# Expert feed-forward of a two-layer backbone block: whole tiles as two-part operands with three products, and a new split of the experts into rounds

## The chip, the core and the metric

The kernel runs on one core of a Trainium2 chip. The metric is the device time of one execution in microseconds (us), shown as the median of several runs. Engines are named as the profile names them: PE (TensorE, matmuls; PEld its weight loads), DVE (VectorE), ACT (ScalarE), POOL (GpSimd), SP (SyncE, which here issues the large loads). PE's clock has two levels, 1.2 and 2.4 GHz; the profile gives the granted share of the higher one.

## The reference

A block of two layers over 256 latent tokens and 256 context tokens of width 1024, all in 32-bit floats. Each layer mixes tokens and then channels. In the second layer the channel mixer, for the latent tokens alone, is a mixture of eight experts, of which each token uses two:

```python
def swiglu(h, wg, wu, wd):
    return (jax.nn.silu(h @ wg) * (h @ wu)) @ wd

def moe_swiglu(h, router_w, router_b, wg, wu, wd):
    logits = h.astype(jnp.float32) @ router_w.astype(jnp.float32) + router_b.astype(jnp.float32)
    top_val, top_idx = lax.top_k(logits, TOP_K)                     # TOP_K = 2
    ...
    for e in range(N_EXPERTS):                                      # 8
        out = out + gates[..., e:e + 1] * swiglu(h, wg[e], wu[e], wd[e])
```

An expert has three matrices of 1024 x 3584 floats (`wg`, `wu`, and `wd` the other way round), so that the eight experts' weights are 8 x 3 x 1024 x 3584 x 4 bytes = 352.3 MB. They are read once. The change is in this mixture alone.

## The kernel before

All the work up to the router is left as it is. `moe` (in class `K`) computes the router, sorts the experts by how many tokens chose them (expert 0 has most), and hands over to class `Experts`.

**Tiles.** The token slots of the sorted experts are cut into quads of 32 slots. Four quads make a tile of 128 slots; `TILES` (L1323) lists six of them as pairs (expert, first slot). A tile whose four quads belong to one expert is a whole tile; the others are mixed. There are three whole tiles (128 slots of experts 0, 1 and 2) and three mixed ones. `gather` fetches the tokens of three tiles at once by products with a 0/1 matrix `P` and leaves them transposed in `he`, where they serve as PE's stationary operand.

**Rounds, steps, stages and groups.** `ROUNDS` (L1325) puts three tiles into each of two rounds. `ORDER` walks through the four quarters c of the inner width 3584 (896 columns each) and, in each, through round 0 and round 1: eight steps. A `step` has three stages. Gate and up have four groups (i) each; a group loads 256 rows x 896 columns of the quarter for every expert of the round and multiplies them into six PSUM banks `gu`, two per tile. Then the product `a` of both is transposed seven times per tile (`trans`, PSUM tiles `tr`, result `aT`). Down has four groups (u), the last of half size, again into six banks `gu`, which are added to `acc` (128 x 1024 per tile). After the last quarter `back` scales `acc` by the tokens' gates, splits it into two parts `oh` and `ol`, and multiplies these with `PT` back into token order, onto `ymoe` (24 products for three tiles). `end` does the last norm and writes the output.

**Products.** The weights are the moving operand. `products` (L1453) issues, for a whole tile, one 32-bit product per bank of 448 columns (gate, up) or 512 (down), and for a mixed tile four products per bank, one for each quad, on 32 columns of the array each. In the trace a 32-bit product is two matmul instructions.

**What sets the order.** PE's instructions stand as the loops write them (a manual schedule). ACT's and DVE's are placed by a scheduler, and each engine keeps its own order: an instruction that waits holds up those behind it. SP issues the loads in the order of the loops, into a ring of `NW` = 13 buffers `wf` of 8 KB per partition; a load waits until the last reader of its buffer is done, and for the load eight before it. Round 0 loads three experts per group (0, 1, 7), round 1 five (4, 5, 2, 3, 6).

**Elsewhere in the kernel** the two-part form is in use already: `split` (L102) copies a tile into a rounded part `hi` on ACT (L103) and leaves the rest `lo` on DVE (L104), both of the type fp32r, and `mm3` (L106) issues three products, hi x hi, hi x lo and lo x hi (L108 to L110), one matmul instruction each.

Of the kernel before, what the change touches and what calls it, by code (L numbers as in the profile page):

```python
# [1317 lines left out]
class Experts:  # L1318
# [41 lines left out]
    def gather(self, pool, tiles, h2, ps, he):  # L1360

        nc, k, V = self.nc, self.k, self.nc.vector
        n = sum(32 * len(t) for t in tiles)
        P = self.select(pool, tiles)
        for kk in range(8):
            p = ps(kk)
            i = 0
            for t in range(2):
                for part in range(2):
                    k.mm(p[:, 0:n], h2[part][:, t, 128 * kk:128 * kk + 128], P[:, t], i == 0, i == 3)  # L1370
                    i += 1
            if kk % 2:
                V.tensor_copy(he[:, kk], p[:, 0:n])
            else:
                nc.scalar.activation(he[:, kk], p[:, 0:n], AF.Copy)
        out, c = [], 0
        for i, quads in enumerate(tiles):
# [13 lines left out]
            out.append(dict(quads=quads, m=m, he=he[:, :, c:c + m], PT=pt[0:m], g=g[0:m]))  # L1391
# [3 lines left out]
    def start(self, pool, h2, ps):  # L1395
        T = self.k.T
        self.y = T(self.mp, [128, 2, D], "ymoe")
        self.nc.gpsimd.memset(self.y, 0.0)
        self.he = T(self.mp, [128, 2, 8, 384], "he")
        self.tiles = []  # L1400
        for i in range(2):
            self.tiles += self.gather(pool, self.TILES[3 * i:3 * i + 3], h2, ps, self.he[:, i])


    def go(self, ep, pp):
        nc, k = self.nc, self.k
        self.ep, self.pp = ep, pp
        self.ev, self.acc = {}, {}
        rounds = [[self.tiles[i] for i in r] for r in self.ROUNDS]
        with k.tc.manual_schedule(engines={mybir.EngineType.PE}):  # L1410
            for r, c in self.ORDER:
                self.step(rounds[r], c)
        self.end()
        with k.tc.If(nc.values_load(self.en[0:1, 8:9], min_val=0, max_val=8) > 0):
            for quads in self.MORE:
                q, s0 = quads[0]
                cnt = nc.values_load(self.en[0:1, q:q + 1], min_val=0, max_val=S)
                with k.tc.If(cnt > s0):
# [7 lines left out]
                    for c in range(4):  # L1426
                        self.step(tiles, c)
            self.end()

    NW = 13  # L1430
# [14 lines left out]
    def down_weights(self, q, c, u):  # L1445
# [5 lines left out]
        return [w[:, 512 * i:512 * i + 512] for i in range(n)]  # L1451

    def products(self, p, cols, tile, lhs, rhs, first, last):  # L1453

        quads = tile["quads"]
        if len(quads) == 4 and len({q for q, s in quads}) == 1:
            for ps, r in zip(p, rhs[quads[0][0]]):
                self.k.mm(ps[:, 0:cols], lhs, r, first, last)
            return
        for i, ps in enumerate(p):  # L1460
            for j, (q, s0) in enumerate(quads):
                js = slice(32 * j, 32 * j + 32)
                self.k.mm(ps[js, 0:cols], lhs[:, js], rhs[q][i], first, last)

    def step(self, tiles, c):
# [4 lines left out]
        a = [self.T([128, 896], "a", bufs=3) for t in tiles]  # L1470
        for up in range(2):
            ps = banks()
            for i in range(4):
                w = {q: self.up_weights("moe_w_up" if up else "moe_w_gate", q, c, i) for q in experts}
                for t, p in zip(tiles, ps):
                    for kk in range(2):
                        self.products(p, 448, t, t["he"][:, 2 * i + kk], {q: [w[q][kk][:, 448 * s:448 * s + 448] for s in range(2)] for q in w},
                                      i + kk == 0, i + kk == 4)
            for t, p, o in zip(tiles, ps, a):
                m = t["m"]  # L1480
                for s in range(2):
# [12 lines left out]
        for t, p in zip(tiles, ps):
# [85 lines left out]
```

## Time and profile before

| | us |
|---|---|
| median of 3 runs (2483.76 to 2494.44) | 2490.39 |
| the profiled execution, device time | 2495.73 |
| its span, first to last instruction | 2494.0 |
| of it the experts' products, first to last | 1516.6 to 2466.6 |
| of it the last tiles' way back, the norm and the output | 2466.6 to 2494.0 |

The profile is of one execution. Busy times are what an engine's instructions covered. Matmuls overlap in PE, so that what a matmul costs there is the distance from one start to the next, not its duration. A wait in one engine costs something only where that engine holds up the end.

### The profile page before, as it was taken

To read this page: it belongs to the slowest core of one execution; us is meant where nothing else is said; L and a number is where in the kernel's file an instruction comes from. 1 tells how busy PE (TensorE), PEld (TensorE's weight loads), DVE (VectorE), ACT (ScalarE), POOL (GpSimd) and SP (SyncE) were. 2 spreads that over 40 slices of the span, in tenths; PEclk is the share of its full clock that TensorE was granted. 3 is DMA by queue.
4 is the path that set the end of the run, shared out by engine and by line. 5 is a ranking of instruction groups with operands and counts; after the bars stand their busy time and mean duration, and the time that the engine had idled before them with its cause. 6 is when DMAs were issued, how large, how long until landed. Compare 5 with 4: busy or idle time off the path is not lost.

```text
span 2494.0 us, 40273 instructions
## 1 busy us (share of the span) xinstructions
PE 2197.1 (88%) x16243; PEld 1380.5 (55%) x16243; DVE 1024.7 (41%) x2026; ACT 683.9 (27%) x1438; POOL 258.4 (10%) x385
## 2 busy tenths in 40 slices
PE   5898887699799988988776769999999999999996
PEld 2887545577689967767554545433433343334332
DVE  3575758787543436975476651000010101000203
ACT  2643324454433236553432321010100000000001
POOL 4222231220000002020322020000000000000000
PEclk7999968699989989988886769999999999999998
DMA  8764664434433325425653027899979997999795
GB/s 294 205 171 131 201 228 145 123 123 138 137 99 93 94 85 153 145 81 159 214 199 106 31 85 288 316 381 414 407 280 405 415 408 280 406 413 382 270 409 235
DMA packets 320701, 570.49 MB, mean 229 GB/s; under 512 B 25422, under 2 KB 208474, under 8 KB 301562
## 3 DMA queue, kind: packets, MB, share of 16 engines
q1 hardware_dynamic: 303786, 544.46, 60.7%
q10 hardware_dynamic: 12816, 15.42, 1.8%
q0 software_dynamic: 3904, 7.94, 0.9%
q8 instruction: 130, 2.13, 0.4%
q14 instruction: 65, 0.53, 0.1%
HBM read 546.71 MB, written 21.05 MB: 228 GB/s over the span
## 4 chain that ended last, share of the span: by engine, by line
PE 40%; DMA 9%; DVE 5%; ACT 2%; issue 1%; POOL 1%; SPq 0%; ACTq 0%; DVEq 0%; POOLq 0%
PE gu L113 30%; DMA wf<-in_moe_w_down 5%; PE z L113 3%; DMA wf<-in_moe_w_up 2%; DMA lo<-in_ada_w 1%; PE ada L113 1%; PE he L113 1%; PE tr L116 1%; DVE T L1009 0%; DVE itmp L1007 0%; DVE A L999 0%; PE lora L113 0%; PE o L108 0%; PE A L113 0%; PE gu L108 0%
## 5 line engine op out<-in xcount | busy, mean ns | idle before, releaser
L113 PE MATMUL gu<-wf,he 128*32 128x448 f32 (+1 forms) x3840 | 604.2, 542 | 0.2
L113 PEld LDWEIGHTS gu<-wf,he 128*32 128x32 f32 (+1 forms) x3840 | 235.6, 126 | 367.5 <-issue 355.2
L113 PE MATMUL gu<-wf,aT 128*32 128x512 f32 (+1 forms) x1680 | 303.7, 596 | 1.0 <-DMA wf<-in_moe_w_down 1.0
L1484 DVE TENSOR_TENSOR a<-a,gu 128x448 f32<-128x448 f32 x48 | 29.8, 621 | 657.9 <-PE gu L113 655.7
L113 PEld LDWEIGHTS gu<-wf,aT 128*32 128x32 f32 (+1 forms) x1680 | 105.1, 126 | 193.3 <-issue 187.7
L113 PE MATMUL z<-hi,wf 128*128 128x256 f32 x736 | 175.1, 392 | 5.3 <-ACT u L640 5.1
L113 PEld LDWEIGHTS z<-hi,wf 128*128 128x128 f32 x736 | 139.4, 194 | 31.2 <-ACT u L640 5.5
L104 DVE TENSOR_TENSOR wl<-wf,wh 128x512 fp32r<-128x512 f32 (+1 forms) x167 | 128.6, 772 | 61.5 <-ACT wh L103 57.0
L103 ACT ACTIVATE wh<-wf 128x512 fp32r<-128x512 f32 (+1 forms) x167 | 114.5, 688 | 131.9 <-PE gu L109 53.4
L1486 ACT ACTIVATE a<-gu 128x448 f32<-128x448 f32 x48 | 26.0, 543 | 398.5 <-PE gu L113 398.5
L1503 DVE TENSOR_TENSOR acc<-acc,gu 128x512 f32<-128x512 f32 x36 | 24.4, 686 | 225.1 <-PE gu L113 224.9
L1516 ACT ACTIVATE aT<-tr 128x512 f32<-128x512 f32 (+1 forms) x48 | 23.5, 541 | 312.7 <-PE tr L116 312.7
L1557 POOL TENSOR_TENSOR wf<-wf,ol 128x512 f32<-128x512 f32 x2 | 3.3, 1646 | 990.6 <-DVE ol L1556 990.6
L108 PE MATMUL gu<-hi,wh 128*128 128x256 f32 x320 | 96.1, 300 | 7.2 <-ACT wh L103 6.2
L110 PE MATMUL gu<-hi,wl 128*128 128x256 f32 x320 | 96.0, 300 | 5.7 <-DVE wl L104 5.6
L109 PE MATMUL gu<-lo,wh 128*128 128x256 f32 x320 | 93.6, 292 | 0.0
L1009 DVE TENSOR_TENSOR T<-T,itmp 64x31 f32<-64x31 f32 (+15 forms) x248 | 88.2, 356 | 6.1
L104 DVE TENSOR_TENSOR bk<-wf,bk 128x512 fp32r<-128x512 f32 x72 | 49.8, 692 | 96.6 <-ACT bk L103 95.5
L1007 DVE TENSOR_TENSOR itmp<-A,T 64x31 f32<-64x31 f32 (+15 forms) x248 | 84.4, 340 | 5.6
L749 ACT ACTIVATE ltmp<-win,Q 128x128 f32<-128x128 f32 x176 | 64.3, 395 | 63.7 <-DMA win<-zd 20.4
L113 PE MATMUL A<-ar,bk 64*128 64x128 f32 (+1 forms) x512 | 60.7, 308 | 18.3 <-POOL bk L843 16.6
L103 ACT ACTIVATE bk<-wf 128x512 fp32r<-128x512 f32 x72 | 45.3, 629 | 100.1 <-PE gu L109 60.9
(506 smaller groups left out, 3867.2 us busy)
## 6 DMA issues: line engine op xcount, KB each, us to landing
wf<-in_moe_w_gate SPq DMA_DIRECT2D x128, 896.0 KB, 12.3
wf<-in_moe_w_up SPq DMA_DIRECT2D x128, 896.0 KB, 16.4
wf<-in_moe_w_down SPq DMA_DIRECT2D x96, 1024.0 KB, 18.0
wf<-in_w_in SPq DMA_DIRECT2D x75, 512.0 KB, 4.4
lo<-in_ada_w SPq DMA_DIRECT2D x28, 1024.0 KB, 5.6
wf<-in_ffn_w_gate SPq DMA_DIRECT2D x32, 512.0 KB, 3.7
wf<-in_ffn_w_up SPq DMA_DIRECT2D x32, 512.0 KB, 3.8
wf<-in_ffn_w_down SPq DMA_DIRECT2D x32, 512.0 KB, 3.6
```

Source lines behind the costliest of these rows:

```text
L103: self.nc.scalar.activation(hi, src, AF.Copy)
L104: (eng or self.nc.vector).tensor_tensor(lo, src, hi.bitcast(F32), op=OP.subtract)
L108: mm(ps, lhsT=lh, rhs=rh, start=first, stop=False)
L109: mm(ps, lhsT=lh, rhs=rl, start=False, stop=False)
L110: mm(ps, lhsT=ll, rhs=rh, start=False, stop=last)
L113: self.nc.tensor.matmul(ps, lhsT=l, rhs=r, start=start, stop=stop)
L116: self.nc.tensor.transpose(ps, src, self.ident[0:n, 0:n])
L749: self.nc.scalar.activation(tmp[pt], w[pt, 1:129], AF.Copy, scale=self.Q[pt, i:i + 1])
L1007: V.tensor_tensor(tv, A32[:, i + 1:32, i:i + 1].to_broadcast([64, n, m]), T32[:, i:i + 1, 0:m].to_broadcast([64, n, m]), op=OP.mult)
L1009: V.tensor_tensor(T32[:, i + 1:32, 0:m], T32[:, i + 1:32, 0:m], tv, op=OP.subtract)
L1484: V.tensor_tensor(o_, o_, p[s][0:m, 0:448], op=OP.mult)
L1486: nc.scalar.activation(o_, p[s][0:m, 0:448], AF.Silu)
```

## The change

It touches only class `Experts`.

- **Tiles and rounds.** The whole tiles are still the first 128 slots of experts 0, 1 and 2. The mixed ones are now (0, 0, 6, 7), (1, 3, 3, 3) and (4, 4, 5, 5). Round 0 is whole 0, mixed, whole 2 with experts 0, 6, 7, 2; round 1 is mixed, whole 1, mixed with experts 1, 3, 4, 5. Both load four experts per group.
- **Two parts.** `gather` keeps a whole tile's tokens in two parts of type fp32r. A whole tile's weights are split when they are used (`parts`: buffers `wh` and `wl`, three of each), and its `aT` too. `products` then issues three fp32r products in place of one 32-bit product. Mixed tiles are multiplied as before, from the unsplit weights.
- **Buffers.** `NW` goes from 13 to 8.
- **Order.** A bank is evicted right behind its tile's last product, not behind the whole stage. `trans` and the products of `back` are put into a list `todo` and run behind the products of the next tile. `back` takes its parts from `wh` and `wl`.

```diff
-    TILES = [[(0, 0), (0, 32), (0, 64), (0, 96)], [(1, 0), (1, 32), (1, 64), (1, 96)], [(0, 128), (0, 160), (1, 128), (7, 0)],
-    ROUNDS = [(0, 1, 2), (3, 4, 5)]
+    TILES = [[(0, 0), (0, 32), (0, 64), (0, 96)], [(2, 0), (2, 32), (2, 64), (2, 96)], [(0, 128), (0, 160), (6, 0), (7, 0)],
+    ROUNDS = [(0, 2, 1), (4, 3, 5)]
...
-    NW = 13
+    NW = 8
...
+    def parts(self, w, n):
+
+        hi, lo = [self.T([128, 1024], t, F32R, 3)[:, 0:n] for t in ("wh", "wl")]
+        self.k.split(hi, lo, w)
+        return hi, lo
...
     def products(self, p, cols, tile, lhs, rhs, first, last):
-        if len(quads) == 4 and len({q for q, s in quads}) == 1:
-            for ps, r in zip(p, rhs[quads[0][0]]):
-                self.k.mm(ps[:, 0:cols], lhs, r, first, last)
+        if self.whole(quads):
+            for l, r in ((0, 0), (1, 0), (0, 1)):
+                for i, ps in enumerate(p):
+                    mm(ps[:, 0:cols], lhs[l], rhs[r][:, cols * i:cols * i + cols], first and l == r, last and r == 1)
             return
...
     def step(self, tiles, c):
+        turn = lambda t, w, j, n: self.parts(w[t["quads"][0][0]][j], n) if self.whole(t["quads"]) else {q: w[q][j] for q in w}
...
+                for n, (t, p, o) in enumerate(zip(tiles, ps, a)):
+                    late = len(self.todo)
                     for kk in range(2):
+                        self.products(p, 448, t, [x[:, 2 * i + kk] for x in t["he"]], turn(t, w, kk, 896), i + kk == 0, i + kk == 4)
+                    self.flush(late)
+                    if i == 3:
...
+                        if up:
+                            self.todo.append(lambda n=n, t=t, o=o: aT.update({n: self.trans(t, o)}))
...
-            if c == 3:
-                self.back(t, self.acc[key][0:m])
+                    if c == 3:
+                        self.todo += self.back(t, self.acc[key][0:m])
...
     def back(self, t, acc):
+        def products(n, oh, ol):
...
+            oh, ol = [self.T([128, 1024], x, F32R, 3)[:, 0:512] for x in ("wh", "wl")]
...
+            out.append(lambda n=n, oh=oh, ol=ol: products(n, oh, ol))
+        return out
```

How the instructions stand now, at three places.

PE, round 0, gate, first group: the two whole tiles and the first rows of the mixed one. `wf` are weight buffers, `gu` PSUM banks (L113 is the helper `mm`). Before:

```order
L113 MATMUL gu_14023<-wf_14029,he_13800 128x448
L113 MATMUL gu_14024<-wf_14029,he_13800 128x448
L113 MATMUL gu_14023<-wf_14029,he_13800 128x448
L113 MATMUL gu_14024<-wf_14029,he_13800 128x448
L113 MATMUL gu_14025<-wf_14040,he_13800 128x448
L113 MATMUL gu_14026<-wf_14040,he_13800 128x448
L113 MATMUL gu_14025<-wf_14040,he_13800 128x448
L113 MATMUL gu_14026<-wf_14040,he_13800 128x448
L113 MATMUL gu_14027<-wf_14029,he_13800 32x448 x2
L113 MATMUL gu_14027<-wf_14040,he_13800 32x448
```

Now, the same place up to the mixed tile:

```order
L113 MATMUL gu_14108<-wh_14158,he_2610_13801 128x448
L113 MATMUL gu_14109<-wh_14158,he_2610_13801 128x448
L113 MATMUL gu_14108<-wh_14158,he_2611_13802 128x448
L113 MATMUL gu_14109<-wh_14158,he_2611_13802 128x448
L113 MATMUL gu_14108<-wl_14159,he_2610_13801 128x448
L113 MATMUL gu_14109<-wl_14159,he_2610_13801 128x448
L113 MATMUL gu_14108<-wh_14168,he_2610_13801 128x448
L113 MATMUL gu_14109<-wh_14168,he_2610_13801 128x448
L113 MATMUL gu_14108<-wh_14168,he_2611_13802 128x448
L113 MATMUL gu_14109<-wh_14168,he_2611_13802 128x448
L113 MATMUL gu_14108<-wl_14169,he_2610_13801 128x448
L113 MATMUL gu_14109<-wl_14169,he_2610_13801 128x448
```

A whole tile's four 32-bit products of a group have become twelve fp32r products, the last two of each six from the part that DVE makes, and the mixed tile comes next instead of the second whole tile.

ACT, the end of the first gate stage. `a` is the result of the stage, made from the banks of the three tiles in turn. Before:

```order
L1486 ACTIVATE a_14020<-gu_14023 128x448
L1486 ACTIVATE a_14020<-gu_14024 128x448
L1486 ACTIVATE a_14021<-gu_14025 128x448
L1486 ACTIVATE a_14021<-gu_14026 128x448
L1486 ACTIVATE a_14022<-gu_14027 128x448
L1486 ACTIVATE a_14022<-gu_14028 128x448
```

Now (L103 is the first half of `split`; `wh_14390` and `wh_14400` are the second whole tile's weights of the last gate group, `wh_14426` and later those of the up stage):

```order
L1516 ACTIVATE a_14105<-gu_14108 128x448
L1516 ACTIVATE a_14105<-gu_14109 128x448
L1516 ACTIVATE a_14106<-gu_14110 128x448
L103 ACTIVATE wh_14390<-wf_14348 128x896
L103 ACTIVATE wh_14400<-wf_14348 128x896
L1516 ACTIVATE a_14106<-gu_14111 128x448
L103 ACTIVATE wh_14426<-wf_14418 128x896
L103 ACTIVATE wh_14436<-wf_14418 128x896
L1516 ACTIVATE a_14107<-gu_14112 128x448
L1516 ACTIVATE a_14107<-gu_14113 128x448
```

The splits of the weights that the second whole tile needs now stand behind an eviction that waits for the mixed tile's first bank.

PE, round 0, last quarter: where the way back of the first tile (`tr<-...PT`) stands. Before:

```order
L113 MATMUL gu_17502<-wf_17593,aT_17485 32x512 x2
L113 MATMUL gu_17502<-wf_17595,aT_17485 32x512
L113 MATMUL gu_17502<-wf_17597,aT_17485 32x512
L113 MATMUL tr_17617<-oh_17613,PT_13871 128x512
L113 MATMUL tr_17617<-ol_17614,PT_13871 128x512
L113 MATMUL tr_17621<-oh_17613,PT_13871 128x512
L113 MATMUL tr_17621<-ol_17614,PT_13871 128x512
```

Now:

```order
L113 MATMUL gu_19531<-wf_19745,aT_19514 32x512
L113 MATMUL tr_19777<-wh_19761,PT_13913 128x512
L113 MATMUL tr_19777<-wl_19762,PT_13913 128x512
L113 MATMUL tr_19781<-wh_19761,PT_13913 128x512
L113 MATMUL tr_19781<-wl_19762,PT_13913 128x512
L113 MATMUL tr_19785<-wh_19765,PT_13913 128x512
L113 MATMUL tr_19785<-wl_19766,PT_13913 128x512
L113 MATMUL tr_19789<-wh_19765,PT_13913 128x512
L113 MATMUL tr_19789<-wl_19766,PT_13913 128x512
L113 MATMUL gu_19532<-wh_19803,aTh_19562 128x512
```

Before, all 24 products stood behind the step's last product; now the first tile's eight stand between the mixed tile's last product and the second whole tile's last ones, whose weights come from the same ring `wh`.

## Rows read from the trace of the kernel before

**Rows 1.** The page: busy time by engine, and two lines of slices:

```profile
PE 2197.1 (88%) x16243; PEld 1380.5 (55%) x16243; DVE 1024.7 (41%) x2026; ACT 683.9 (27%) x1438; POOL 258.4 (10%) x385
PE   5898887699799988988776769999999999999996
DMA  8764664434433325425653027899979997999795
```

**Rows 2.** Busy us by stretch: PE, PEld, DVE, ACT, POOL; PEclk, DMA share, GB/s:

```profile
1752.60:1868.60 116.00, 115.25 (x581) 47.57 (x581) 7.09 (x11) 6.79 (x13) 0.00 (x0) 1.00 0.86 339
1868.60:1988.10 119.50, 118.36 (x853) 43.20 (x845) 7.92 (x13) 6.20 (x12) 0.00 (x0) 1.00 1.02 410
2339.80:2350.10 10.30, 7.31 (x28) 3.65 (x24) 10.01 (x17) 2.89 (x4) 0.00 (x0) 1.00 0.99 393
2466.60:2494.00 27.40, 7.38 (x28) 3.62 (x24) 17.27 (x27) 7.14 (x15) 3.29 (x2) 0.75 0.12 42
```

**Rows 3.** The same view: round 0's gate and up, its down; then round 1's:

```profile
1752.60:1827.40 74.80, 74.80 (x388) 31.13 (x384) 3.01 (x5) 3.86 (x7) 0.00 (x0) 1.00 1.01 405
1831.40:1868.60 37.20, 37.20 (x174) 13.59 (x176) 3.36 (x5) 0.86 (x2) 0.00 (x0) 1.00 0.58 214
1868.60:1944.90 76.30, 76.23 (x581) 27.36 (x573) 3.83 (x7) 3.26 (x6) 0.00 (x0) 1.00 1.03 406
1949.00:1988.10 39.10, 38.78 (x253) 12.99 (x252) 3.43 (x5) 0.74 (x2) 0.00 (x0) 1.00 1.01 416
```

**Rows 4.** Matmuls in 32 bits: min/median/max ns; whole tiles in order of time (start, us):

```profile
L113 PE MATMUL gu<-wf,he x3840: 538/539/644, 1516.6 to 2424.6; 128*32 128x448 f32 x148, 128*128 128x448 f32 x44
L113 PE MATMUL gu<-wf,aT x1680: 592/592/697, 1596.0 to 2466.1; 128*32 128x512 f32 x146, 128*128 128x512 f32 x41
1564.46 5.42 PE L113 MATMUL gu<-wf,he 128*128 128x448 f32 x14
1596.82 5.74 PE L113 MATMUL gu<-wf,aT 128*128 128x512 f32 x13
```

**Rows 5.** Busy time by stretch, earlier: fp32r products of 512, then 256 columns:

```profile
741.20:763.40 22.20, 22.20 (x97) 17.95 (x97) 9.13 (x15) 7.06 (x14) 0.00 (x0) 1.00 0.31 94
763.60:808.40 44.80, 44.80 (x384) 44.80 (x383) 16.26 (x29) 15.21 (x31) 0.00 (x0) 1.00 0.31 95
```

**Rows 6.** Groups by line and shape: xcount | busy us, mean ns | idle before:

```profile
L103 ACT ACTIVATE wh<-wf 128x512 fp32r<-128x512 f32 x144 | 90.5, 629 | 110.3 <-PE gu L109 53.4 <-PE dn L110 27.9 <-PE o L110 8.4
L103 ACT ACTIVATE wh<-wf 128x1024 fp32r<-128x1024 f32 x23 | 24.1, 1051 | 21.5 <-PE z L109 21.5
L104 DVE TENSOR_TENSOR wl<-wf,wh 128x512 fp32r<-128x512 f32 x144 | 100.4, 699 | 42.6 <-ACT wh L103 38.3 <-POOL u L689 3.2
L104 DVE TENSOR_TENSOR wl<-wf,wh 128x1024 fp32r<-128x1024 f32 x23 | 28.2, 1230 | 18.8 <-ACT wh L103 18.8
```

**Rows 7.** The same view, from 1510 us on: evictions and way back:

```profile
L1486 ACT ACTIVATE a<-gu 128x448 f32<-128x448 f32 x48 | 26.0, 543 | 398.5 <-PE gu L113 398.5
L1503 DVE TENSOR_TENSOR acc<-acc,gu 128x512 f32<-128x512 f32 x36 | 24.4, 686 | 225.1 <-PE gu L113 224.9
L1533 DVE TENSOR_TENSOR ymoe<-ymoe,tr 128x512 f32<-128x512 f32 x24 | 15.3, 678 | 0.6 <-PE tr L113 0.6
L1527 DVE SCALAR_TENSOR_TENSOR ol<-acc,gs,oh 128x512 fp32r<-128x512 f32 x12 | 8.9, 744 | 0.0
L1526 ACT ACTIVATE oh<-acc,gs 128x512 fp32r<-128x512 f32 x12 | 8.7, 722 | 78.8 <-DVE acc L1503 65.9 <-PE tr L113 12.6
```

**Rows 8.** Loads from 1495 us on: KB each, median us to landing:

```profile
wf<-in_moe_w_gate SPq DMA_DIRECT2D x128, 896.0 KB, 12.3
wf<-in_moe_w_down SPq DMA_DIRECT2D x96, 1024.0 KB, 18.0
```

**Rows 9.** The first loads, 1495 to 1530 us, and one wait of SP (longest last):

```profile
DMA to landing us min/median/max: 4.8/12.9/17.5
SPq L1442 <- PE he L113: 14.5, 1, 14.5
```

More of the change, by code (lines that the diff above doesn't have):

```diff
@@ L1390, in gather @@
             V.tensor_copy(g[0:m], p[0:m, 256:257])
-            out.append(dict(quads=quads, m=m, he=he[:, :, c:c + m], PT=pt[0:m], g=g[0:m]))
+            rows = [x[:, :, c:c + m] for x in parts] if self.whole(quads) else [he[:, :, c - nw:c - nw + m]]
+            out.append(dict(quads=quads, m=m, he=rows, PT=pt[0:m], g=g[0:m]))
             c += m
@@ L1398, in start @@
         self.nc.gpsimd.memset(self.y, 0.0)
-        self.he = T(self.mp, [128, 2, 8, 384], "he")
         self.tiles = []
         for i in range(2):
-            self.tiles += self.gather(pool, self.TILES[3 * i:3 * i + 3], h2, ps, self.he[:, i])
+            tiles = self.TILES[3 * i:3 * i + 3]
+            n = sum(map(self.whole, tiles))
+            he = T(self.mp, [128, 8, 384 - 128 * n], f"he{i}")
+            parts = [T(self.mp, [128, 8, 128 * n], f"he{i}{j}", F32R) for j in range(2)]
+            self.tiles += self.gather(pool, tiles, h2, ps, he, parts)
     def go(self, ep, pp):
@@ L1462, in products @@
                 js = slice(32 * j, 32 * j + 32)
[L1463 removed]
+                mm(ps[js, 0:cols], lhs[0][:, js], rhs[q][:, cols * i:cols * i + cols], first, last)
     def step(self, tiles, c):
@@ L1515, in trans @@
                 k.tr(p[:, m * j:m * j + m], a[0:m, j0 + j::7], m)
[L1516 to L1517 removed]
+            src = p[:, 0:m * n].rearrange("p (j m) -> p j m", m=m)
+            if whole:
+                k.split(o[0][:, j0:j0 + n, 0:m], o[1][:, j0:j0 + n, 0:m], src)
+            else:
+                nc.scalar.activation(o[0][:, j0:j0 + n, 0:m], src, AF.Copy)
+        return [x[:, :, 0:m] for x in o]
     def back(self, t, acc):
         nc, V, m = self.nc, self.nc.vector, t["m"]
[L1522 removed]
+        def products(n, oh, ol):
             ns = slice(512 * n, 512 * n + 512)
[L1524 to L1527 removed]
             for h in range(2):
@@ L1533, in back @@
                 V.tensor_tensor(self.y[:, h, ns], self.y[:, h, ns], p, op=OP.add)
+        out = []
+        for n in range(2):
+            ns = slice(512 * n, 512 * n + 512)
+            oh, ol = [self.T([128, 1024], x, F32R, 3)[:, 0:512] for x in ("wh", "wl")]
+            nc.scalar.activation(oh[0:m], acc[:, ns], AF.Copy, scale=t["g"])
+            V.scalar_tensor_tensor(ol[0:m], acc[:, ns], t["g"], oh[0:m].bitcast(F32), op0=OP.mult, op1=OP.subtract)
+            out.append(lambda n=n, oh=oh, ol=ol: products(n, oh, ol))
+        return out
     def end(self):
```

102 lines of the change are left out of this document (57 added, 45 removed).

## The prediction

> **What bounds the kernel now.** I read the page first [rows 1]. From the 25th slice on, which is the experts' part, PE is at 9 tenths throughout; the line of DMA below it swings there between 5 and 9. So in this part PE is the bound and the loads have room, at least in some stretches. The view by stretch [rows 2] shows in which. Round 0's step of the second quarter takes 116.0 us at 339 GB/s, round 1's 119.5 us at 410 GB/s with a DMA share of 1.02; the other three quarters are pairs of the same kind. PE is busy for all but one us of each. Stage by stage [rows 3], round 1 takes 1.5 us longer in gate and up (76.3 against 74.8) and 1.9 us in down (39.1 against 37.2), with as many products: these 3.4 us are the waits for loads, since round 1 loads five experts and round 0 three. So a pair of steps is 232 us of PE work and some 3.4 us of waits. Loads alone, at 410 GB/s, would need 88.1 MB / 410 = 215 us a pair. PE is the bound, and the loads stand 17 us below it.
>
> **What the change does to PE.** Starts of 32-bit products lie (5.42 - 0.54) / 13 = 0.376 us apart at 448 columns and (5.74 - 0.59) / 12 = 0.429 us at 512 [rows 4], from the stretch less the last one's own length (0.539 and 0.592 us, same rows). A product is two of them: 0.752 and 0.858 us. fp32r products lie 22.2 / 96 = 0.231 us apart at 512 columns and 44.8 / 384 = 0.117 us at 256 [rows 5]; between them, at 448, 0.203 us. Three cost 0.608 and 0.694 us. A whole tile has 32 bank products in gate and up and 14 in down per step, so it saves 32 x 0.144 + 14 x 0.164 = 6.9 us, of some 36. A mixed tile is left as it is. Round 0 keeps two whole tiles and round 1 one, so that the PE work of a step falls from 116.0 to 102.2 us in round 0 and from 116.1 to 109.2 in round 1: 83 us over four quarters, if nothing else ended later.
>
> The Trainium skill ("FP8 and Floating Point Precision", TensorE Precision Notes) says that true FP32 takes four passes through the array; three of four would save 9.0 us per whole tile and step, 25 us more in all than the rows give. The rows decide: 0.608 is 0.81 of 0.752, not 0.75. By the page the time would be some 8 us lower, because only round 1 is still paced by PE.
>
> **The loads.** Both rounds now load four experts: 44.0 MB a step, at 410 GB/s [rows 2] 107.4 us. That is more than round 0's PE work and a little less than round 1's. So the new split takes the waits out of round 1 and makes the loads the pace of round 0. The ring has 8 buffers in place of 13, two groups of four. In round 0 a group is whole, mixed, whole; its PE work is 2 x 2.43 + 3.0 + 0.3 = 8.2 us (the 0.3 is what 74.8 us [rows 3] hold beyond 96 products of 0.752, over eight groups) against 3.67 MB / 410 = 9.0 us for the loads. Experts 0, 6 and 7 are held until the mixed tile is done, 5.7 us into the group, and expert 2 until DVE has split it. A single load took 4.8 us from issue to landing at the least [rows 9], and each that queues behind it 2.2 us more. So the three land 10.5, 12.7 and 14.9 us into the group, or 2.2 later behind an earlier load of expert 2, and are wanted two groups on: the first at 16 us (18 less its split), the others at 20.6, behind the whole tile. That leaves 3 us or more, and the loads can keep running; but 3 us is not much, and stalls of both sides will meet.
>
> **Splits.** A pass of 896 columns is copied by ACT and subtracted by DVE. Between the rows for 512 and 1024 columns [rows 6] that is 0.95 and 1.10 us; at 1024 1.05 and 1.23. PE uses a pass of 896 for 6 x 0.203 = 1.22 us, so that DVE alone would just keep up, and in a group of round 0 it has 4 x 1.10 = 4.4 us of work in 9. They are hidden by the mixed tile and by three buffers, wherever the order lets them run ahead. Where it doesn't, PE waits. At the end of round 0's gate the second whole tile's split stands behind an eviction of the mixed tile's first bank; that bank ends 0.75 us before the tile, the eviction takes 0.54 [rows 7], the split 0.95, then DVE's 1.10: 1.1 us late at the end. Likewise 0.6 us at the end of down, and at the start of each round 0 the evictions into `acc` (0.69 each) hold up DVE's first split by 1.0 us. Scattered transposes add changes between PE's modes: taken as 0.6 us in round 0 and 0.5 in round 1. So 2.3 us in round 0 and 1.5 in round 1.
>
> **The steps.** Round 0: PE 104.5, loads 107.4; I take 107.4. Round 1: PE 110.7, plus half of the 3.4 us that the waits cost where loads run at full rate: 112.4. Half, because PE and not DMA is the longer there, but by little. A pair is 219.8 us, four are 879.2.
>
> **Ways back.** Before, 24 products with their waits took 10.3 us after round 0 and as much of the tail after round 1 [rows 2]. Now they lie between other tiles. Round 0: 24 x 0.231 = 5.5 us of PE, and 4 us in which the second whole tile's last weights wait for the ring `wh`: PE must release the first tile's parts, which need two additions, two `ol` and two `ymoe` on DVE [rows 7], then ACT and DVE split. Together 9.5, so nothing is won there. Round 1: 16 x 0.231 = 3.7 us and 3.7 us of the same wait. Sum 16.9 us.
>
> **Start and tail.** The first product waits for `gather`, as before; its columns are the same in number (1536 per slice of the width), so I leave 1516.6 us and add 1.5 for the first split, whose DVE half stands behind the last copies of `gather`. Before, SP's second load waited 14.5 us for `gather` [rows 9]; now the first eight loads wait for buffers that are free by then, so that two groups are there when PE begins. That is no gain by itself, since PE is not waiting there. Tail: of the 27.4 us [rows 2] 11.0 were three ways back; one is left, bound by DVE: 2 x 0.69 + 2 x 0.74 + 4 x 0.68 = 5.6. So 22.0.
>
> **Sum.** 1516.6 + 1.5 + 879.2 + 16.9 + 22.0 = 2436.2 us of span, against 2494.0. The profiled execution took 1.7 us more than its span, so 2437.9, and lay 5.3 us above the median of the runs: **2433**.
>
> **Rivals.**
> *Clean overlap.* If cushions hold everywhere and only the loads pace round 0 and only PE round 1, a pair is 107.4 + 109.2: 13 us less, 2420. If even the loads are hidden, PE's 211.4 a pair is all: 34 less, 2399. For it: round 1 of before lost only 3.4 us in twelve groups with its loads at full rate. Against: that was with 13 buffers.
> *Exposed splits.* If the loads come just in time, each group's first split lies open: 0.95 + 1.10 us less the four high products (0.81), 1.24 us. In the 46 groups of one round that is 57 us: 2490, no change; in a quarter of them, 2447. Against: the 3 us above, and ACT and DVE are at half load.
> *Too few buffers* (the slower side). A buffer's cycle is its use, its landing and its split: 5.7 + L + 2.05 us, and it must fit into two groups, 18 us. The median landing was 12.3 us for gate and 18.0 for down [rows 8], because eight loads queue in SP's ring; if L stays 13 with the ring of 8, a group takes 10.4 us, 1.0 over its mean of 9.3 (107.4 / 11.5), and 92 groups cost 95 us: 2528. It decides from L = 12 us on, where the 57 us are gone. Against: with four buffers in use only four can queue, and L is 4.8 to 9.2.
> *It doesn't do what it says.* If fp32r products of 448 columns between 32-column tiles cost as much as the two 32-bit ones, nothing is saved: pairs of 118.3 + 119.3, 2504.
> *Slow loads.* Busy stretches move 405 to 416 GB/s [rows 3]; if four experts a group ran at the 339 of round 0's whole step, each step would be 130 us: 2594. That 339 holds idle time (214 in down, 0.58 busy), so I give it 0.01. The Trainium skill ("DMA: Bandwidth & Descriptors", Specifications) puts a core's share of HBM at about 358 GB/s, which would make the weights alone 984 us, longer than the stage is now; the trace disagrees, with 410 over 119.5 us.
>
> **How the numbers follow.** Forecast 0.65, with 2412 to 2456 as its own range (from near-clean overlap to 3.4 us of waits in each step). Clean overlap 0.12, exposed splits 0.12, too few buffers 0.07, no saving 0.03, slow loads 0.01. The range takes in most of clean overlap and the first part of exposed splits: 2402 to 2482. Half a per cent is about what a measurement of this kernel can tell: faster means under 2478, slower over 2503. Faster: 0.65 + 0.12 + 0.06 = 0.83; same 0.07, from exposed splits and part of no saving; slower 0.10.
>
> **What would show it.** In the trace after: starts of fp32r products of 448 columns 0.20 us apart; steps near 107 and 112 us in place of 116.0 and 119.5; a DMA share near 1.0 in both rounds; loads from 1500 us on without a gap; a stall of some 4 us before the last products of round 0's second whole tile; the end 22 us behind the last product of `gu`. It is wrong if PE waits over 0.5 us per group on `wh`, `wl` or `wf`, if landing takes over 12 us, or if DMA falls well under 400 GB/s inside a stage.

## The result and the profile after

| | before | after |
|---|---|---|
| median, us | 2488.6 (2483.76 to 2494.44, 4 runs) | 2426.89 (2414.86 to 2437.87, 4 runs) |
| ratio, 95% interval | | 0.975 (0.9707 to 0.9793) |
| profiled execution: span | 2494.0 | 2418.1 |
| first product of the experts at | 1516.6 | 1504.6 |
| products of `gu`, first to last | 950.0 | 888.5 |
| tail behind them | 27.4 | 25.0 |

The changed kernel takes 2427 us; 2433 was forecast. Of the 75.9 us between the two spans, 12.0 lie ahead of the experts' first product, where the two kernels differ in `gather`, the first split and the start of the loads (10507 and 10540 matmul instructions), and the last section shows that this part differs from one execution of the same kernel to the next. So the reading below goes by what is called the stage from here on, from the first product of `gu` to the end of the span: **977.4 us before, 913.5 after**, 63.9 less.

The page after; it answers to [rows 1]:

```profile
PE 2112.2 (87%) x16827; PEld 1483.1 (61%) x16827; DVE 1336.8 (55%) x2342; ACT 939.5 (39%) x1730; POOL 258.8 (11%) x385
PE   4898877799879988988965677999999999999996
DMA  8765574444433316434655024999999999999994
```

Before, the DMA line swung between 7 and 9 in the experts' part (the 5 is the last slice, which holds the tail); now it stands at 9 from the 26th slice to the last but one (the experts begin at the end of the 25th). PE's line reads the same as before, and that is the trap of this case. The steps of the second quarter, those of the last, and the tail, by stretch, with the columns of [rows 2]:

```profile
1723.90:1829.59 105.69, 103.91 (x666) 64.07 (x666) 58.36 (x61) 49.66 (x60) 0.00 (x0) 1.00 1.02 408
1829.59:1940.49 110.90, 110.90 (x896) 53.41 (x895) 33.94 (x38) 27.27 (x35) 0.00 (x0) 1.00 1.02 405
2158.36:2275.41 117.05, 111.81 (x686) 69.04 (x682) 67.86 (x76) 50.99 (x63) 0.00 (x0) 0.97 1.02 407
2275.41:2393.13 117.72, 114.70 (x913) 53.84 (x912) 41.73 (x50) 30.72 (x39) 0.00 (x0) 0.99 0.85 332
2393.13:2418.10 24.97, 6.13 (x16) 3.38 (x16) 13.96 (x21) 5.76 (x13) 3.20 (x2) 0.65 0.12 46
```

A pair of steps is 216.6 us in place of 235.5. By the first two rows round 1 looks as if PE were its bound: busy for all of 110.90 us. The runs show that it isn't.

Products of 448 columns stand as forecast, six in 1.21 us, by the timeline of one whole tile (start, length, instructions):

```profile
1514.58 0.97 PE L113 MATMUL gu<-wh,he 128*128 128x448 f32 x4
1515.38 0.57 PE L113 MATMUL gu<-wl,he 128*128 128x448 f32 x2
1515.79 0.97 PE L113 MATMUL gu<-wh,he 128*128 128x448 f32 x4
```

### The profile page after: what moved, and what is told of

Its sections match the earlier page's. It is cut to its first block, busy times and chain, and to the rows that moved or that the text cites. A ratio compares the mean times of both kernels' runs of the same rounds, so it can differ in the third digit from the quotient of the medians.

```text
span 2418.1 us, 42430 instructions
## 1 busy us (share of the span) xinstructions
PE 2112.2 (87%) x16827; PEld 1483.1 (61%) x16827; DVE 1336.8 (55%) x2342; ACT 939.5 (39%) x1730; POOL 258.8 (11%) x385
## 4 chain that ended last, share of the span: by engine, by line
PE 39%; DMA 8%; DVE 7%; ACT 4%; issue 2%; POOL 1%; SPq 0%; ACTq 0%; DVEq 0%; POOLq 0%
PE gu L113 28%; DMA wf<-in_moe_w_up 5%; PE z L113 3%; DVE wl L104 1%; ACT wh L103 1%; DMA lo<-in_ada_w 1%; PE he L1372 1%; DMA win<-zd 1%; PE tr L116 1%; PE gu L108 1%; ACT ltmp L749 1%; DVE T L1009 1%; PE gu L110 0%; DVE itmp L1007 0%; PE gu L109 0%
## 5 line engine op out<-in xcount | busy, mean ns | idle before, releaser
L104 DVE TENSOR_TENSOR wl<-wf,wh 128x896 fp32r<-128x896 f32 (+2 forms) x443 | 430.9, 994 | 494.1 <-ACT wh L103 481.1
L103 ACT ACTIVATE wh<-wf 128x896 fp32r<-128x896 f32 (+2 forms) x443 | 374.2, 869 | 562.9 <-DMA wf<-in_moe_w_up 158.0
L113 PE MATMUL gu<-wf,he 128*32 128x448 f32 x3072 | 314.5, 542 | 0.1
L113 PEld LDWEIGHTS gu<-wf,he 128*32 128x32 f32 x3072 | 107.6, 110 | 172.9 <-issue 157.0
L113 PE MATMUL gu<-wh,he 128*128 128x448 f32 x768 | 194.6, 375 | 4.6 <-ACT wh L103 4.0
L113 PE MATMUL z<-hi,wf 128*128 128x256 f32 x736 | 176.4, 394 | 5.7 <-ACT u L640 5.5
L113 PEld LDWEIGHTS gu<-wh,he 128*128 128x128 f32 x768 | 139.5, 188 | 60.9 <-issue 27.3
L113 PEld LDWEIGHTS z<-hi,wf 128*128 128x128 f32 x736 | 140.2, 195 | 32.0 <-ACT u L640 6.1
L113 PE MATMUL gu<-wf,aT 128*32 128x512 f32 x1344 | 151.7, 595 | 0.0
L113 PE MATMUL gu<-wl,he 128*128 128x448 f32 x384 | 111.9, 373 | 3.5 <-DVE wl L104 2.9
L113 PEld LDWEIGHTS gu<-wf,aT 128*32 128x32 f32 x1344 | 40.0, 110 | 89.8 <-issue 87.8
L103 ACT ACTIVATE bk<-wf 128x512 fp32r<-128x512 f32 x72 | 45.3, 629 | 100.1 <-PE gu L109 60.9
L113 PEld LDWEIGHTS gu<-wl,he 128*128 128x128 f32 x384 | 70.8, 189 | 16.1 <-DVE wl L104 10.6
L113 PE MATMUL A<-ar,bk 64*128 64x128 f32 (+1 forms) x512 | 56.6, 298 | 20.5 <-POOL bk L843 17.5
## 6 DMA issues: line engine op xcount, KB each, us to landing
wf<-in_moe_w_up SPq DMA_DIRECT2D x128, 896.0 KB, 12.9
wf<-in_moe_w_down SPq DMA_DIRECT2D x96, 1024.0 KB, 12.3
```

The source lines that it names most:

```text
L103: self.nc.scalar.activation(hi, src, AF.Copy)
L104: (eng or self.nc.vector).tensor_tensor(lo, src, hi.bitcast(F32), op=OP.subtract)
L113: self.nc.tensor.matmul(ps, lhsT=l, rhs=r, start=start, stop=stop)
```

## The experiments

The time of the second quarter's steps, of `gu` and of the stage come from one profile each; times with an interval come from interleaved runs, and their ratio is to the kernel before in the same series (2488.6 to 2498.0 us). e3_two leaves out one product of three; e4_half and e11_order_half load about half of the weights.

| | time, us | ratio (95%) | steps of the second quarter, round 0 and 1 | gu | stage |
|---|---|---|---|---|---|
| before | 2488.6 | | 116.0, 119.5 | 950.0 | 977.4 |
| after | 2426.9 | 0.975 (0.9707 to 0.9793) | 105.7, 110.9 | 888.5 | 913.5 |
| e10_after, after once more | 2429.8 | 0.974 (0.9708 to 0.9771) | 105.9, 110.9 | 886.8 | 911.0 |
| e1_products | 2485.1 | 0.9977 (0.9949 to 1.0004) | 101.2, 129.5 | 946.0 | 970.3 |
| e2_split | 2488.5 | 0.9995 (0.9965 to 1.0024) | 116.3, 116.6 | 946.9 | 974.2 |
| e3_two | 2410.9 | one run | 106.0, 110.2 | 871.3 | 895.9 |
| e4_half | 2391.8 | one run | 100.9, 108.5 | 858.9 | 883.3 |
| e5_ring6 | 2475.4 | 0.9909 (0.9877 to 0.9940) | 113.2, 114.9 | 926.5 | 950.5 |
| e6_order | 2454.9 | 0.9855 (0.9791 to 0.9919) | 111.8, 114.7 | 911.5 | 939.9 |
| e7_before_ring8 | 2539.7 | one run | 116.0, 130.9 | 993.3 | 1020.6 |
| e8_back | 2425.5 | 0.973 (0.9683 to 0.9776) | 105.8, 110.6 | 881.8 | 906.2 |
| e9_spread | 2432.2 | 0.973 (0.9698 to 0.9763) | 105.7, 110.9 | 881.2 | 906.1 |
| e11_order_half | 2436.6 | one run | 104.5, 110.4 | 875.5 | 903.8 |

### Each part alone

The products without the new split (in the changed kernel):

```diff
-TILES: [0 x4] [2 x4] [0 0 6 7] | [1 x4] [1 3 3 3] [4 4 5 5]
+TILES: [0 x4] [1 x4] [0 0 1 7] | [2 x4] [4 4 5 5] [3 3 3 6]
 ROUNDS = [(0, 2, 1), (4, 3, 5)]
```

> The changed kernel with the old split of the tiles: round 0 holds experts 0, 1 and 7 with two whole tiles, round 1 the experts 4, 5, 2, 3 and 6 with one; products, ring, order as changed. Bytes: 33.0 MB in a step of round 0, 55.05 MB in one of round 1. Theory (the prediction's: PE saves 20.7 us a pair, but only the new split lets the loads follow): round 0 is PE's, 104 to 105 us; round 1 is the loads', 55.05 MB / 410 = 134 us, less what the ring of eight has loaded ahead (up to 8 x 2.2 us, of which I take 6), 128; a pair 232 against the changed kernel's 218, so about 2484, no change against before. Rival (the products alone do it, the split is decoration): a pair of 104.5 + 111 = 215.5, 2425.

The new split without the products (in the kernel before):

```diff
-TILES: [0 x4] [1 x4] [0 0 1 7] | [4 4 5 5] [2 x4] [3 3 3 6]
+TILES: [0 x4] [2 x4] [0 0 6 7] | [1 x4] [1 3 3 3] [4 4 5 5]
-ROUNDS = [(0, 1, 2), (3, 4, 5)]
+ROUNDS = [(0, 2, 1), (4, 3, 5)]
```

> The kernel before with the new split and order of the tiles alone: both rounds load four experts; 32-bit products, 13 buffers, transposes and ways back as before. Theory: PE stays the bound with 116 us a step in both rounds, and only round 1's 3.4 us of waits for loads go: steps of 116 and 116.3, 13 us in all, about 2475. Rival (the waits come from the 410 GB/s that round 1 has anyway, and stay): steps 116 and 119.5, 2488. Rival (the split is the larger part of the gain): under 2460.

By stretch, round 0 and round 1 of the second quarter, first of e1_products, then of e2_split:

```profile
1770.33:1871.57 101.24, 101.20 (x665) 64.14 (x665) 60.10 (x61) 51.13 (x59) 0.00 (x0) 1.00 0.89 341
1871.57:2001.05 129.48, 119.58 (x897) 53.52 (x896) 33.63 (x38) 26.45 (x35) 0.00 (x0) 1.00 1.02 410
```

```profile
1748.78:1865.07 116.29, 115.53 (x578) 47.35 (x574) 7.17 (x11) 6.79 (x13) 0.00 (x0) 1.00 0.95 377
1865.07:1981.64 116.57, 115.81 (x850) 41.78 (x849) 7.85 (x12) 6.19 (x12) 0.00 (x0) 1.00 0.98 381
```

The first came out as the theory had it, 2485 for 2484. Round 0 wins 14.8 us with its cheaper products, and round 1 loses 9.9: at 410 GB/s and a share of 1.02 it can only wait for its five experts, while the loads stand still for a tenth of round 0. The second removes round 1's waits (119.5 to 116.6) and is then held by PE in both rounds. Its first step took 121.7 us, so that the stage is 3.2 us shorter and the time unchanged within its interval; 2475 was expected. Alone the parts bring 7.1 and 3.2 us of the stage (the second is hardly more than the 2.4 by which the stage of one kernel differs between two executions, e10_after), together 63.9. Each takes away one of two bounds that lie close together. But the parts are not taken apart cleanly: e1_products keeps the changed kernel's order and its ring of 8 buffers, and 8 buffers alone cost the kernel before 43 us with this old split (e7_before_ring8, below). What the products would bring with the old split and 13 buffers, no run shows.

### What paces the rounds now

Less work for PE, then fewer bytes (both in the changed kernel):

```diff
-            for l, r in ((0, 0), (1, 0), (0, 1)):
+            for l, r in ((0, 0), (1, 0)):
```

> The changed kernel with two products in place of three for whole tiles: the product of the activations' high part with the weights' low part is left out (the splits are still made). PE has 9.7 us less work per whole tile and step: 19.4 us in round 0, 9.7 in round 1. Theory (loads pace round 0, PE round 1): round 0 stays at 106 to 108 us, round 1 falls from 111 to the loads' 107; the products of gu span 888.5 - 16 = 872 us. Rival B (loads pace both rounds already): both stay, 885 to 889. Rival C (PE, with its waits for splits, paces both): round 0 falls to 87, round 1 to 101, 773.

```diff
-        src = ...[256 * i:256 * i + 256, ...]; dma_start(v, src...); return [v[:, 0], v[:, 1]]
+        src = ...[256 * i:256 * i + 128, ...]; dma_start(v[:, 0], src); return [v[:, 0], v[:, 0]]
```

> The changed kernel with about half the bytes: each load of gate and up brings only its first 128 rows, each of down its first 1024 columns, and they are used twice, so that PE, ACT and DVE do all that they did. 23.1 MB a step in place of 44.0, some 57 us of transfer. Theory: round 0 falls from 106.5 to PE's 102.2 + 2.3 of stalls = 104.5, round 1 from 111.3 to 110.7, or to 109.5 if waits for loads are in it; the products of gu span 875 to 880 us. Rival B (loads pace both rounds): round 1 falls by as much as round 0, both by 3 us or more, under 865. Rival C (splits and order pace both): both stay, 885 to 889.

The second quarter's steps of e3_two, then of e4_half:

```profile
1724.11:1830.14 106.03, 95.20 (x577) 46.40 (x574) 57.06 (x60) 48.15 (x60) 0.00 (x0) 1.00 1.02 409
1830.14:1940.39 110.25, 106.60 (x850) 42.63 (x850) 34.80 (x39) 28.68 (x37) 0.00 (x0) 1.00 1.02 408
```

```profile
1717.65:1818.59 100.94, 100.94 (x669) 64.21 (x665) 59.23 (x60) 51.12 (x60) 0.00 (x0) 1.00 0.68 231
1818.59:1927.09 108.50, 108.50 (x896) 50.27 (x895) 35.31 (x39) 28.79 (x36) 0.00 (x0) 1.00 0.63 212
```

With 29 us less PE work in a pair, the pair takes 216.3 us in place of 216.6. So the loads pace **both** rounds: rival B by the steps of e3_two, although its `gu` of 871.3 is the 872 of the theory, by another way. The steps of 105.7 and 110.9 run at nearly the same rate and differ in where the border falls (105.69 x 408 = 43.1 MB against 110.90 x 405 = 44.9, together the pair's 88.0). Of the 17.2 us that `gu` did lose, 14.0 are in the first step (101.2 for 107.3) and the last (109.8 for 117.7); in these two the loads of after stand at a share of 0.94 and 0.85. e4_half gives PE's own pace: 100.9 and 108.5, 209.4 a pair, 7 us below the loads' (with the order of ACT and DVE that the scheduler made for it, of which more below). Its `gu` of 858.9 is rival B's (under 865), but round 1 falls by 2.4 us, not by the 3 or more that B wanted.

That ACT and DVE with their splits are not the pace either shows in what ACT waited for in after, from 1500 us on (us in total, times, longest):

```profile
ACT wh L103 <- DMA wf<-in_moe_w_up: 158.0, 40, 8.1
ACT wh L103 <- DMA wf<-in_moe_w_gate: 118.5, 31, 8.3
ACT wh L103 <- DMA wf<-in_moe_w_down: 79.7, 23, 8.0
```

Why did PE look busy in round 1? The last mixed tile of one group and the first of the next (64 instructions in a row), by the timeline, in after, in e4_half and in e3_two:

```profile
1853.91 6.57 PE L113 MATMUL gu<-wf,he 128*32 128x448 f32 x64
```

```profile
1833.19 6.22 PE L113 MATMUL gu<-wf,he 128*32 128x448 f32 x64
```

```profile
1855.89 7.27 PE L113 MATMUL gu<-wf,he 128*32 128x448 f32 x64
```

The same work takes 6.22 us in all seven such places of e4_half's step, 6.5 to 6.9 us in after's and 7.3 to 8.2 in e3_two's. Mixed tiles need no split and PE's order is the same in after and e4_half, so the difference is the wait for a late load, and in after all of it counts as busy: it lies between the products and leaves no idle time. The seven places together are 2.6 us longer in after than in e4_half, the step 2.4.

The idle time that the profile does name is another matter. The waits of PE in the second quarter of after (waits by engine and line: us in total, times, longest):

```profile
PE gu L113 <- ACT wh L103: 1.4, 2, 0.7
PE gu L113 <- DVE wl L104: 0.6, 1, 0.6
```

In e4_half that list is empty for the same quarter. That doesn't make them waits for late loads, since the scheduler places ACT's and DVE's instructions anew for each kernel, and in e4_half it has put the splits earlier. The two waits on ACT, at the start of round 0's step and at the end of its gate, in after:

```profile
1722.41 0.60 ACT L1536 ACTIVATE acc<-gu 128x512 f32<-128x512 f32 x1 [0.17 <-PE gu L113]
1722.91 1.78 ACT L103 ACTIVATE wh<-wf 128x896 fp32r<-128x896 f32 x2
1723.90 1.09 PE L113 MATMUL gu<-wh,he 128*128 128x448 f32 x4 [0.70 <-ACT wh L103]
1753.96 0.54 ACT L1516 ACTIVATE a<-gu 128x448 f32<-128x448 f32 x1 [1.65 <-PE gu L113]
1754.40 1.78 ACT L103 ACTIVATE wh<-wf 128x896 fp32r<-128x896 f32 x2
1755.40 1.07 PE L113 MATMUL gu<-wh,he 128*128 128x448 f32 x4 [0.75 <-ACT wh L103]
```

The second place in e4_half (the later of the second whole tile's two last splits of the gate, and the mixed tile's first eviction):

```profile
1744.58 0.95 ACT L103 ACTIVATE wh<-wf 128x896 fp32r<-128x896 f32 x1 [0.26 <-PE gu L113]
1747.41 0.54 ACT L1516 ACTIVATE a<-gu 128x448 f32<-128x448 f32 x1 [1.01 <-PE gu L113]
```

In after both splits start the moment that the eviction ahead of them is done, and the load for the first (issued at 1711.5 us, landed 6.3 us later) had been there for 5 us. These are waits for ACT's order. The third, of 0.59 us on DVE at the start of down, is not taken apart here. They do not set the pair's length, which e3_two keeps.

### The ring

```diff
-    NW = 8
+    NW = 6
```

> The changed kernel with 6 buffers in the ring of the loads in place of 8. Theory (the prediction's rival of too few buffers, with its own rule): use 5.7 us + landing + splits 2.05 us must fit into 6/4 of a group; with landings of 4.8 to 9.2 us a group takes 8.4 to 11.3 us, 9.8 in the middle, 0.75 over the 9.05 us that a group now takes; over 92 groups +70 us, about 2497. Rival (the ring is deep enough, the 407 GB/s alone set the pace): steps as in the changed kernel, 2427 to 2435.

And the kernel before:

```diff
-    NW = 13
+    NW = 8
```

> The kernel before with 8 buffers in its ring in place of 13. Theory: round 1's loads need 134 us for 116 us of PE work, and what closes the gap is what 13 buffers hold in advance, 29 us; with 8 it is 17.6, 11 us less, so that round 1's steps go from 119.5 to 130 and round 0's stay at 116: +42 us, about 2532. Rival (the ring does not matter where PE is the bound): steps of 116 and 119.5, 2490.

The second quarter, of e5_ring6 and of e7_before_ring8:

```profile
1743.53:1856.71 113.18, 109.21 (x665) 65.66 (x666) 58.08 (x61) 48.35 (x59) 0.00 (x0) 1.00 0.99 391
1856.71:1971.61 114.90, 112.76 (x896) 55.17 (x895) 34.44 (x39) 27.38 (x37) 0.00 (x0) 1.00 0.98 383
```

```profile
1764.21:1880.21 116.00, 115.25 (x578) 47.57 (x577) 7.06 (x11) 6.79 (x13) 0.00 (x0) 1.00 0.78 298
1880.21:2011.12 130.91, 123.39 (x854) 45.47 (x846) 7.96 (x13) 6.19 (x12) 0.00 (x0) 1.00 1.02 410
```

Two buffers fewer cost 37 us of stage (950.5 for 913.5), half of what the rival's rule gave: the rate falls from 406 to 387 GB/s. In the kernel before, 8 buffers cost 43 us, 42 expected: five experts a group need more than 8 (what lies between 8 and 13 was not tried). With 8 buffers and the new products the old split takes 970.3 us of stage (e1_products), the even one 913.5. So the change could give up five buffers because its rounds are even.

### The order

Transposes between up and down, ways back behind the whole step, as before; then the same with half the bytes:

```diff
-                    self.flush(late)          # behind each tile's products
+        self.flush()                          # once, behind up
+        for t in tiles: self.todo += self.back(t, ...); self.flush()     # c == 3, behind down
```

> The changed kernel with the old places of transposes and ways back: all transposes of a step between its up and its down, all ways back behind the whole step; split, products and ring as changed. Theory (after the runs with half the loads and with two products: both rounds go at the pace of the loads, and PE has 5.3 us of room in round 0 and 2.4 in round 1): the exposed wait of the last tile's transposes and of the first tile's split costs 2 to 3 us a step, of which room hides half; 8 x 1.2 = 10 us; way back of round 0 as before 10.3; round 1's 6.4 leaves its step, but the tail grows by two ways back, 9 us; together +12, about 2439. Rival (loads hide it all): +3, 2430. Rival (nothing is hidden): 8 x 3 + 3 = +27, 2454.

> The run with the old places of transposes and ways back, with about half the bytes as in the run with half the loads. Theory (a wait of PE between up and down fills the ring, the loads stop, and what they lose is not caught up, since they set the pace): PE alone takes 100.9 + 3.1 of wait + some 3 us at half clock = 106 to 107 us in round 0 and 110 in round 1, both under the 111.6 and 113.5 with all the bytes, and round 0's under the loads' own 107.4. Rival (the wait is PE's, and PE is the bound): as with all the bytes, 111 to 113.

e6_order at its border of up and down, by the timeline (in brackets the idle time before and its releaser), and two stretches:

```profile
1807.25 3.59 PE L116 MATMUL tr<-k_ident,a 128*128 128x128 f32 x14 [3.07 <-DVE aTl L104]
```

```profile
1807.20:1813.00 5.80, 5.70 (x20) 4.81 (x21) 2.27 (x4) 3.53 (x6) 0.00 (x0) 0.50 1.02 424
1831.00:1841.00 10.00, 10.00 (x64) 5.74 (x66) 3.86 (x4) 3.24 (x4) 0.00 (x0) 1.00 0.52 187
```

e11_order_half, second quarter:

```profile
1747.66:1852.19 104.53, 101.47 (x670) 64.22 (x666) 59.23 (x60) 51.39 (x61) 0.00 (x0) 1.00 0.67 223
1852.19:1962.58 110.39, 109.03 (x896) 50.27 (x895) 35.22 (x39) 28.48 (x35) 0.00 (x0) 1.00 0.63 208
```

The old order costs 26.4 us of stage, all of what the rival "nothing is hidden" gave; my 12 fell. PE alone needs 104.5 and 110.4 in that order, 214.9 a pair and still less than the loads' 216.3, yet with all the bytes the pair takes 226.5. The rows show how: PE waits 3.07 us, runs the next 5.8 us at a granted clock of 0.50 (the lower level), and some 18 us later the loads are down to a share of 0.52 for 10 us. What the loads lose there is not made up, because they are the pace. My 106 to 107 for round 0 counted that half clock in; with half the bytes the clock stayed at 1.00 in that quarter. That the idle loads are the buffers that PE held longer is inferred from the order of events, not tried by itself; e11_order_half, like e4_half, has its own order of ACT and DVE too.

### The ways back

One lent buffer of the ring holds the parts of a way back:

```diff
-            oh, ol = [self.T([128, 1024], x, F32R, 3)[:, 0:512] for x in ("wh", "wl")]
+            oh, ol = b[:, 1024 * n:1024 * n + 512], b[:, 1024 * n + 512:1024 * n + 1024]    # b: one "wf"
```

> The changed kernel with the parts of a way back in a buffer of the ring of the loads (one of 8, both halves) in place of two of the three buffers of each weight part. Theory (the stalls of the last quarter are PE waiting for the weight parts that queue behind a way back): the step of round 0 in the last quarter falls from 117.0 to 113, that of round 1 from 117.7 to 115, gu in all by 6 us, about 2421. Rival (the loads set the end there too, or the lent buffer delays them): 0 to -1, 2426. Rival (the stalls are the additions into ymoe on DVE): at most 2 us, 2425.

Then, besides, round 0's ways back half a tile at a time, and the changed kernel once more:

```diff
-                        self.todo += self.back(t, self.acc[key][0:m])
+                        self.slow += [(t, self.acc[key][0:m], h) for h in range(2)]   # round 0
+                    self.drip()          # behind each tile: the products of one half, the scaling of the next
```

> The run with lent buffers, and besides the ways back of round 0 spread: half a tile at a time, one half behind each of the next six tiles, with one pair of buffers of their own; the last round's as in that run. Theory (what is left of round 0's way back is PE waiting for scaling and for the additions into ymoe, 4.8 us of waits beside 5.5 us of products): the first step of the last quarter falls from 115.3 to 110, the last one takes over a third of the products, 116.5; gu in all from 881.8 to 878, the stage from 906 to 902.5; some 2419 with a start at 1512. Rival (the loads stand at their pace there, and PE's gain goes into waiting for them): stage 906.

> The changed kernel itself once more, beside the others of this call. Theory (the stage of the experts repeats within 2 us, and what differs between executions of one kernel lies ahead of it): stage 912 to 915, first product of the experts anywhere from 1504 to 1518. Rival (the stage itself varies, and with it the differences read from single profiles): outside 910 to 917.

The last quarter's steps of e8_back, then of e9_spread:

```profile
2169.30:2284.65 115.35, 108.37 (x686) 66.95 (x682) 67.76 (x76) 52.43 (x64) 0.00 (x0) 1.00 0.99 395
2284.65:2399.50 114.85, 112.88 (x913) 52.98 (x912) 41.25 (x50) 28.50 (x37) 0.00 (x0) 1.00 0.92 359
```

```profile
2183.49:2295.46 111.97, 106.30 (x678) 65.90 (x674) 64.26 (x69) 50.02 (x61) 0.00 (x0) 1.00 1.02 408
2295.46:2411.84 116.38, 114.81 (x921) 54.45 (x920) 44.88 (x57) 31.06 (x41) 0.00 (x0) 1.00 0.91 353
```

e8_back takes 6.7 us off `gu` against after's profile and 5.0 against e10_after's (6 expected), 1.7 and 2.9 us of the 6.7 in the last two steps (115.35 and 114.85 where 113 and 115 were expected, so that round 0 gained less than half of what the theory gave it). Its stage of 906.2 us, with e9_spread's 906.1, is the shortest of the kernels that do all the work. In whole times it can't be told from after (ratios of 0.973 and 0.974). e9_spread gains 3.4 us in round 0's last step and gives 1.5 back in the next; with the other steps nothing is left: the rival. e10_after repeats every step of after within 1.1 us and the stage within 2.5 us, one microsecond beyond what I had called repeating (911.0 where 912 was the edge).

## Why the prediction was right

The time was right to 0.3%; not every reason was, and that it came so close is in part luck: the start alone differs by 11 us between two executions of the changed kernel. The sum beside what was measured, in the profiled executions:

| term | predicted | after | e10_after |
|---|---|---|---|
| first product of the experts (with the first split) | 1518.1 | 1504.6 | 1515.8 |
| eight steps with ways back | 879.2 + 16.9 = 896.1 | 888.5 | 886.8 |
| tail | 22.0 | 25.0 | 24.2 |
| span | 2436.2 | 2418.1 | 2426.8 |

- **PE's saving.** The pace of the products held. PE's work was set a little high: 102.2 and 109.2 us before stalls, 100.9 and 108.5 measured in e4_half.
- **Splits.** The stalls are there, their price is not. Of the 2.3 + 1.5 us, 1.0 + 1.1 + 0.6 were waits for splits; the second quarter of after has 0.70 us at the start of round 0's step and 0.75 at the end of its gate, both by the order on ACT (at the start I had put it on DVE), and 0.59 at the start of down, not at its end. They add nothing to a pair whose length the loads set. The other 1.1 us, for changes of PE's mode, no run shows as a term: e4_half's 100.9 and 108.5 hold all such changes and lie below the bare work that I had put. Exposed splits did not come: all of PE's waits for `wh` and `wl` in the experts' products are 7.3 + 5.3 us, not 57.
- **The loads.** Right for round 0: 44.0 MB a step at 406 to 408 GB/s. The failed step is "PE the pace of round 1". Both rounds are the loads' (216.3 us a pair with 29 us less PE work), and the 112.4 that I built from PE's work, its stalls and half of the old waits came near 110.9 by luck. The rival of clean overlap has the measured pair to the digit, 107.4 + 109.2 = 216.6, and by luck as well, since its second term is PE's work too. The Trainium skill ("DMA: Bandwidth & Descriptors", Specifications) gives about 358 GB/s for a core's share; a pair of steps in after moved 406, so the trace disagrees.
- **Too few buffers.** The mechanism is real (e5_ring6), its criterion was not. I had it decide from a landing of 12 us, and named that as a sign of being wrong; the loads of up and down in after land in 12.9 and 12.3 at the full rate:

```profile
wf<-in_moe_w_up SPq DMA_DIRECT2D x128, 896.0 KB, 12.9
wf<-in_moe_w_gate SPq DMA_DIRECT2D x120, 896.0 KB, 7.7
wf<-in_moe_w_down SPq DMA_DIRECT2D x96, 1024.0 KB, 12.3
```

  In e5_ring6, 37 us slower, they land sooner:

```profile
wf<-in_moe_w_up SPq DMA_DIRECT2D x128, 896.0 KB, 8.7
wf<-in_moe_w_down SPq DMA_DIRECT2D x96, 1024.0 KB, 9.2
```

  The time from issue to landing holds the time in the queue behind other loads. What told the two apart was the share, 1.02 against 0.98 to 0.99, with 406 against 387 GB/s.
- **Ways back.** 16.9 for 10.9 + 6.7 = 17.6 us (117.05 and 117.72 against the means of the second and third quarters, 106.2 and 111.1). In round 1 the wait that I named is there, 2.57 us on `wh` where 3.7 were put. In round 0 it is 0.72 and not 4; besides there are a wait of 1.65 us for `ymoe` and a clock that fell behind both. The timeline, the stretch from there on, and one some microseconds later, where the loads fall to a share of 0.58 as they did in e6_order:

```profile
2266.75 0.47 PE L113 MATMUL tr<-wh,PT 128*128 128x512 f32 x1 [1.65 <-DVE ymoe L1577]
2268.92 1.22 PE L113 MATMUL gu<-wh,aTh 128*128 128x512 f32 x2 [0.72 <-ACT wh L103]
2385.68 0.74 PE L113 MATMUL gu<-wh,aTh 128*128 128x512 f32 x2 [2.57 <-ACT wh L103]
```

```profile
2268.90:2274.70 5.80, 5.72 (x12) 3.64 (x12) 4.54 (x8) 1.44 (x2) 0.00 (x0) 0.52 1.03 407
2278.00:2288.00 10.00, 9.59 (x76) 5.05 (x72) 6.50 (x8) 3.81 (x4) 0.00 (x0) 1.00 0.58 187
```

  The sum came out, not its parts. The products stand later than I counted: 16 of the 48 in round 0's last step, 16 in round 1's and 16 behind the last product of `gu`, where I had 24, 16 and 8. And the very last step is PE's: with half the bytes e4_half takes 117.80 us there as well, 9.3 over its 108.5, so that 6.7 is only what the way back shows over the loads' pace.

- **Tail.** Mis-sized by 3.0 us. The last addition into `ymoe` ends 8.9 us behind the last product of `gu`, not 5.6: the middle tile's way back stands there too (x16 in the tail's row, two ways back where I had one), and PE ran at 0.65 of its clock in the tail.
- **Start.** The 1.5 us for the first split can't be seen in the start, which moves by more than that from one execution to the next.

## What to carry to other kernels

Where two bounds lie 7% apart, a change to one is worth only the distance to the other; judge the parts by what both would be afterwards, and make them together. A busy share of PE proves nothing when its instructions wait inside a group, and a wait that the profile names costs nothing where another bound sets the length: take half of the bytes away and see what is left, and look whether the scheduler has moved the other engines' instructions meanwhile. Once loads set the pace, a stall of PE is not hidden by PE's spare time but only by the buffers, so order and ring depth become worth as much as the arithmetic (26 and 37 us here, of 64).

## What the runs showed of the hardware

- The part ahead of the experts is the same code in after and in its variants (but for the tiles that `gather` fetches in e1_products), yet their first product of `gu` stood anywhere between 1504.6 and 1533.6 us. The mean granted clock up to that product goes with it, roughly: 0.88 for after (1504.6) and e4_half (1506.7), 0.87 for e6_order (1507.8), e3_two (1513.2), e10_after (1515.8) and e8_back (1517.7), 0.86 for e5_ring6 (1515.9), e9_spread (1530.6), e11_order_half (1531.1) and e1_products (1533.6). Between two executions of the same kernel it is the larger difference: 11.1 us between after and e10_after, whose stages differ by 2.4.
- A wait of 3.07 us of PE (e6_order) and one of 1.65 followed by 0.72 (after) were each followed by 5.8 us at the lower level or near it, at a granted clock of 0.50 and 0.52. The place of e6_order's wait had one of 2.74 us in e11_order_half and kept 1.00 over the next 5.8 us; the same wait of 2.74 us in that run's last quarter (at 2247.0 us) was followed by 0.50. What tells them apart was not tried.
